# Block products in the first feed-forward: weight sums that only add, two of four per group made by accumulating transfers

## The chip, the cores and the metric

The kernel runs on one core of one Trainium2 chip. The metric is the device time of one execution in microseconds. Three runs of the kernel before took 991.48, 992.41 and 993.05 us; the median is 992.41 us.

## What is computed

One decoder layer on 512 tokens of width 1024, all in float32: a SwiGLU feed-forward, a token mixer (pooling and dilated attention, gated), a second SwiGLU feed-forward, a final norm. Each of the three is modulated by shifts, scales and gates that come from a condition vector `c` and a 1024 x 9216 matrix. Cut to what matters here:

```python
def swiglu(u, w_in, w_out):
    a, b = jnp.split(u @ w_in, 2, axis=-1)      # w_in 1024 x 5632, w_out 2816 x 1024
    return (jax.nn.silu(a) * b) @ w_out

mod = cond @ w_ada[l] + b_ada[l]                # nine vectors of 1024
u = modulate(rmsnorm(h, g_norm_ffn1[l]), sh1, sc1)
h = h + 0.5 * gt1 * swiglu(u, w_ffn1_in[l], w_ffn1_out[l])
...                                             # token mixer
u = modulate(rmsnorm(h, g_norm_ffn2[l]), sh3, sc3)
h = h + 0.5 * gt3 * swiglu(u, w_ffn2_in[l], w_ffn2_out[l])
return rmsnorm(h, g_final)
```

The change concerns `u @ w_in` of the first feed-forward.

## The kernel before

**Three matmuls for one.** Activations stand transposed (features on partitions, 512 tokens along the row). A float32 number is split into two parts of the type fp32r, `hi` (rounded) and `lo` (the rest), for weights and activations alike, and a product is the sum of `hi*uh`, `hi*ul` and `lo*uh` (`mm3`, L373, and `product`, L758). Every weight is loaded once as a tile of 128 x up to 1024 numbers (512 KB), its `hi` is written by ScalarE (ACT, L331) and its `lo` by VectorE (DVE, L343) into two rings, and TensorE (PE) reads them there.

**Seven products for eight.** For most of `u @ w_in` the kernel takes two column tiles of `a` and two of `b` together, as a group (`duo`, L771). The weights of a group are a 2 x 2 matrix of blocks: the upper and lower half of the 1024 features by `a` and `b`; the activations are a 2 x 2 matrix too, feature halves by token halves. By Winograd's form of Strassen's product seven block products do the work of eight, at the price of sums. Four sums of weight blocks are made per group (from r11, r12, r22, r21), and four sums of activation blocks once per feed-forward (`u_steps`, L717, kept split as `S`). Seven products of 24 matmuls (128 x 256) follow one another on three banks A, B and C; after some of them ACT copies a bank away (L774) before a later product goes on in the same bank: after product 0 it copies A to C, and product 2 writes A again. The banks and these copies are put together at the end (L807, L831), then silu (L790) and the multiplication (L793).

**Stages.** The first feed-forward has 22 tile pairs: 0 to 3 are computed at the start while the norm is still being built, 4 and 5 by plain products, and 6 to 21 as eight groups, two in each of four parts. After each part comes a part of `w_out` (L908 on; L923 adds its result to `H` on DVE). Beside them DVE computes the modulation vectors, one 128 x 1024 product and sum per 128 numbers (`bg`, L419, and L402); their matrix comes in by the same transfers. The mixer has three groups of its own (`gate_duo`), which the change leaves alone. The second feed-forward has nine groups.

**Order.** The order is written out by hand (`manual_schedule`). `plan` (L203) makes one list of all weight tiles in the order of use. An entry names what is to be split: a loaded tile (`raw`), or one of two sum tiles (`x`, two quarters of the tile `X`), and if it is a sum, from which two tiles. `blocks` makes the seven entries of a group. `look` (L353) is called before each product and splits up to three or four entries ahead; `split_hi` issues the sum (`make`, L262, the DVE instruction at L268) and ACT's copy, `split_lo` the DVE subtraction. Each engine works through its own instructions in this order, and waits at the first one that is not ready. SyncE (SP) issues the loads (L251) as buffers become free; in this stage these are three `raw` tiles and two quarters of `X`.

**Two forms of the sums.** `blocks` has a flag. Without it (first feed-forward and mixer) all four sums are DVE instructions: x0 = r12 - r11, x1 = r22 - x0, r12 = r22 - r12, x0 = r21 - x1. With it (second feed-forward) all are additions: x0 = r12 + r11 and x1 = r22 + x0 on DVE, and r12 += r22 and x1 += r21 in place by transfers with addition, issued from GpSimd's queue (POOL, `add`, L272 to L276). The first is issued right behind the making of x1, the second behind the split of r21. The signs are made good by other signs in the activation sums (`u_steps`, L739 to L744) and in the copies and sums behind the products (`sign` and `add`, L775, L807, L822, L828, L831). POOL has no other work in the first feed-forward; it computes the pooling in the mixer and part of the final norm.

Of the kernel before, what the change touches and what calls it, by code (L numbers as in the profile page):

```python
# [12 lines left out]
OP = mybir.AluOpType  # L13
# [126 lines left out]
def chunk_widths():  # L140
    outs = [D] * (KT // 2 * (len(PARTS) - 1)) + [(FT - PARTS[-1][0]) * P] * KT
    f1 = [2 * FIRST * P] * KT + [D] * (2 * (FT - FIRST)), outs
    mix = [D] * 24 + [4 * P] * 2 + ([D] * 4 + [4 * P] * 2) * (KT // 2 - 1) + [D] * KT
    return f1, mix, ([D] * (2 * FT), outs)


class Kernel:
# [6 lines left out]
    def plan(self):  # L154
        (i1, o1), mix, (i2, o2) = chunk_widths()
        self.chunks = []
        for name, ws in (("wf1i", i1), ("wf1o", o1), ("wmix", mix), ("wf2i", i2), ("wf2o", o2)):
            off, rec = 0, []
            for w in ws:
                rec.append((name, off, w))  # L160
                off += P * w
            self.chunks.append(rec)
        f1i, f1o, mx, f2i, f2o = self.chunks


        self.loads, self.order, self.last = [], [], {}
        self.shifted, self.adds = set(), {}

        def plain(recs):
            for r in recs:  # L170
                n = len(self.loads)
                self.loads.append(r)
                self.last[n] = len(self.order)
                self.order.append((r[2], n, ("raw", n), None))

        def blocks(recs, plus=False):
            n = len(self.loads)
            i = len(self.order)
            self.shifted.update(range(len(self.order), len(self.order) + 7))
            self.loads.extend(recs)  # L180
            r11, r12, r22, r21 = (("raw", n + i) for i in range(4))
            x0, x1 = ("x", 0), ("x", 1)
            add = OP.add if plus else OP.subtract
            x2 = x1 if plus else x0
            if plus:
                self.adds[i + 2], self.adds[i + 3] = (r12, r22, True), (x1, r21, False)
            for need, src, make in ((0, r11, None), (1, x0, (x0, r12, r11, add)), (2, x1, (x1, r22, x0, add)), (3, r21, None),
                                    (3, r12, (r12, r22, r12, not plus and add)), (3, r22, None),
                                    (3, x2, (x2, r21, x1, not plus and add))):
                for j, x in enumerate((r11, r12, r22, r21)):  # L190
                    if x == src or (make and x in make):
                        self.last[n + j] = len(self.order)
                self.order.append((D, n + need, src, make))

        def shift(i):

            self.shifted.update(range(len(self.order) - i, len(self.order)))

        def ffn(n, ins, outs, first):
            j, at = first, 0  # L200
            if first:
                plain(ins[:KT])
                at = KT  # L203
            for part, (k0, k1) in enumerate(PARTS):
                while j < pairs_before(n, part):
                    if j < PLAIN[n]:
                        plain(ins[at:at + 2])
                        if n and j < 2:
                            shift(2)
                        j, at = j + 1, at + 2  # L210
                    else:
                        blocks(ins[at:at + 4], n == 2)
                        j, at = j + 2, at + 4
                plain(outs[part * KT // 2:(part + 1) * KT // 2] if part + 1 < len(PARTS) else outs[-KT:])

        ffn(0, f1i, f1o, FIRST)
        shift(4)
        base = len(self.order)
        plain(mx[:26])
        for i in range(26, len(mx) - KT, 6):  # L220
            blocks(mx[i:i + 4])
            plain(mx[i + 4:i + 6])
        plain(mx[-KT:])
        self.shifted.update(range(base, base + 4))
        shift(3)
        ffn(2, f2i, f2o, 0)
        shift(5)
        self.fetched = self.done = self.made = 0

        self.ready = True  # L230
        self.pos, self.held, self.retired, self.half = 0, None, [], None

        self.small, self.smalls = None, []
        self.at, self.start, self.top = {}, {}, 0
        self.buf = {}
        self.units = {base + i: 2 * P for i in (4, 5)}
        self.units.update({base + i: T for i in range(16, 20)})
# [34 lines left out]
    def add(self, i, made):  # L272

        if i in self.adds and self.adds[i][2] == made:
            o, x = (self.source(z) for z in self.adds[i][:2])
            self.nc.gpsimd.dma_start(o, x, accum_op=OP.add)  # L276
# [440 lines left out]
    def u_steps(self, n):  # L717

        nc, v = self.nc, self.nc.vector
        (a11, a12), (a21, a22) = self.U4  # L720

        def add(o, x, y, op):
            return lambda: v.tensor_tensor(o, x, y, op=op)

        def split(i, u):
            x = u if i < 3 else u.rearrange("p (k t) -> p k t", k=4)
            parts = [lambda: nc.scalar.activation(self.S[i][0], x, AF.Copy),
                     lambda: v.tensor_tensor(self.S[i][1], x, self.S[i][0], op=OP.subtract)]
            return parts if n else lambda: [f() for f in parts]

        def whole(u, k):
            x = slice(k, k + 4)
            hi, lo = (y.rearrange("p (k t) -> p k t", k=KT)[:, x, :HT] for y in (self.UHv, self.ULv))
            return lambda: v.tensor_tensor(u.rearrange("p (k t) -> p k t", k=4), hi, lo, op=OP.add)

        def minus(o, x, y):
            return lambda: v.scalar_tensor_tensor(o, x, -1.0, y, op0=OP.mult, op1=OP.subtract)

        if n:  # L739
            adds = [add(a22, a22, a21, OP.subtract), add(a21, a11, a21, OP.subtract), minus(a11, a22, a11),  # L740
                    minus(a12, a12, a11)]
        else:
            adds = [add(a22, a21, a22, OP.add), add(a21, a11, a21, OP.subtract), add(a11, a22, a11, OP.subtract),
                    add(a12, a12, a11, OP.subtract)]  # L744
        return ([whole(a11, 0), whole(a12, 4)] if n else []) + adds, [split(2, a21), split(1, a11), split(0, a22), split(3, a12)]

    def step(self):
# [23 lines left out]
    def duo(self, n, j, first, last, extra):  # L771

        nc, v = self.nc, self.nc.vector
        copy = lambda o, x, f=1.0: nc.scalar.activation(o, x, AF.Copy, scale=f)  # L774
        sign, add = (-1.0, OP.subtract) if n else (1.0, OP.add)  # L775
        T1, T2 = slice(0, HT), slice(HT, T)
        blk = lambda ks, t: [(self.UH[k][:, t], self.UL[k][:, t]) for k in ks]
        lo4, hi4 = range(4), range(4, 8)
# [5 lines left out]
        A, B, C = self.nb(), self.nb(), self.nb()  # L784
        s = self.fw.tile([P, 2 * T], F32, name="sl")
        c = self.fw.tile([P, 2 * T], F32, name="hf")
        u2, u3, p5 = (self.fw.tile([P, T], F32, name=x) for x in ("u2", "u3", "p5"))
        q = lambda x: x.rearrange("p (j h t) -> p j h t", j=2, h=2)
        r = lambda x: x.rearrange("p (j t) -> p j t", j=2)
# [13 lines left out]
        for i, (bank, u, start) in enumerate(((A, blk(lo4, T1), True), (B, S[0], True), (A, S[1], False),  # L803
                                              (C, blk(hi4, T1), False), (A, S[2], False), (B, S[3], False),
                                              (A, blk(hi4, T2), False))):
            if i == 6:
                v.tensor_tensor(q(c)[:, :, 1, :], r(u3), r(p5), op=add)  # L807

            late = i == 2 and n == 0 and j == PLAIN[0]
            if not late:  # L810
                self.look(4)
            self.product(bank, u, start, 0 if i else extra)
            self.step()
            if i == 0:
                copy(C, A)
                if first:
                    first()
                    self.free += self.rawx[:1]
            elif i == 1:
                copy(p5, B)  # L820
            elif i == 2:
                copy(u2, A, sign)  # L822
                if late:
                    self.look(3)
            elif i == 3:
                silu(0, C)
            elif i == 4:
                copy(u3, A, sign)  # L828
            elif i == 6:
                silu(1, A)  # L830
                v.tensor_tensor(q(c)[:, :, 0, :], r(u2), r(B), op=add)  # L831
        if last:
            mult()
            high()
# [983 lines left out]
```

## Time and profile before

| | |
|---|---|
| median of three runs | 992.41 us |
| profiled execution | 992.0 us |
| its span, first to last instruction | 990.2 us |
| granted TensorE clock | 0.999 |
| busy: PE, DVE, ACT, POOL | 979.9, 764.6, 474.6, 45.5 us |
| groups of the first feed-forward | 103.7 to 321.6 us of the span |
| groups of the second feed-forward | 709.4 to 946.4 us |
| transfers with addition | 18, from 697.0 us on |

The profile is one execution, recorded instruction by instruction. Times are microseconds from the first instruction. PE is TensorE's matmuls and PEld its weight loads, which overlap them. A row of a window gives busy time and count of instructions per engine; a row of a timeline gives start, duration, engine, line and operation, output and inputs, and in brackets how long the engine stood idle before and what let it go on. "DMA to landing" runs from the issue of a transfer until its data is there. The line numbers are those of the kernel before.

### The profile page before, as it was taken

How to read it: one execution, taken by the hardware profiler on the slowest of the kernel's cores; microseconds unless marked ns; L12 is line 12 of the kernel's file. 1: busy time of each engine (PE TensorE's matmuls, PEld its weight loads, DVE VectorE, ACT ScalarE, POOL GpSimd, SP SyncE). 2: the span in 40 equal slices, each digit the busy share in tenths (PEclk: the TensorE clock that was granted, in tenths of full speed). 3: DMA queues.
4: the chain of work that ended last, by engine and by line, in shares of the span. 5: the costliest groups of instructions: out<-in, count | busy, mean ns of one | idle time of the engine just before them, and what ended most of it. 6: DMA issues, size and time to landing. Idle time of an engine off the chain costs nothing.

```text
span 990.2 us, 16423 instructions
## 1 busy us (share of the span) xinstructions
PE 979.9 (99%) x6688; PEld 892.8 (90%) x6688; DVE 764.6 (77%) x1072; ACT 474.6 (48%) x712; POOL 45.5 (5%) x49
## 2 busy tenths in 40 slices
PE   8999999999999999999999999999999999999997
PEld 7888998989999899888879998998899898998997
DVE  7989979889797677888879877768676667566653
ACT  5453553525445553446545552455355254352553
POOL 0000000000000000006200000000010000000002
PEclk9999999999999999999999999999999999999999
DMA  9856445465563416654243326513576365563512
GB/s 345 277 184 241 150 149 178 163 192 160 186 205 105 141 57 194 229 184 161 68 122 111 107 81 212 175 44 106 145 194 174 88 175 140 128 184 80 152 34 86
DMA packets 47470, 151.19 MB, mean 153 GB/s; under 512 B 6561, under 2 KB 9377, under 8 KB 47394
## 3 DMA queue, kind: packets, MB, share of 16 engines
q1 hardware_dynamic: 44224, 140.18, 43.4%
q0 software_dynamic: 2592, 9.44, 5.5%
q8 instruction: 52, 0.85, 0.4%
q10 hardware_dynamic: 578, 0.53, 0.2%
q14 instruction: 24, 0.20, 0.1%
HBM read 135.29 MB, written 2.24 MB: 139 GB/s over the span
## 4 chain that ended last, share of the span: by engine, by line
PE 94%; DVE 2%; DMA 1%; SPq 1%; issue 1%; ACT 0%; POOL 0%; POOLq 0%; DVEq 0%; ACTq 0%
PE bank L375 15%; PE bank L376 15%; PE bank L377 15%; PE bank L769 13%; PE bank L768 13%; PE bank L767 13%; PE bank L1744 1%; PE bank L1748 1%; PE bank L1746 1%; SPq L1076 1%; PE bank L1420 1%; PE bank L1122 1%; PE bank L1173 1%; DMA H<-xT 1%; PE bank L1421 1%
## 5 line engine op out<-in xcount | busy, mean ns | idle before, releaser
L343 DVE TENSOR_TENSOR wlo<-raw,whi 128x1024 fp32r<-128x1024 f32 (+4 forms) x162 | 170.6, 1065 | 60.0 <-ACT whi L331 59.8
L767 PE MATMUL bank<-UH,whi 128*128 128x256 f32 x640 | 176.7, 276 | 0.0
L768 PE MATMUL bank<-UL,whi 128*128 128x256 f32 x640 | 176.7, 276 | 0.0
L769 PE MATMUL bank<-UH,wlo 128*128 128x256 f32 x640 | 176.7, 276 | 0.0
L331 ACT ACTIVATE whi<-raw 128x1024 fp32r<-128x1024 f32 (+4 forms) x162 | 146.2, 921 | 39.6 <-DVE raw L268 33.0
L375 PE MATMUL bank<-HI,whi 128*128 128x512 f32 (+1 forms) x406 | 146.2, 360 | 0.0
L376 PE MATMUL bank<-HK,whi 128*128 128x512 f32 (+1 forms) x406 | 145.9, 359 | 0.0
L377 PE MATMUL bank<-HI,wlo 128*128 128x512 f32 (+1 forms) x406 | 145.8, 359 | 0.0
L343 DVE TENSOR_TENSOR wlo<-X,whi 128x1024 fp32r<-128x1024 f32 (+3 forms) x104 | 111.9, 1083 | 39.6 <-ACT whi L331 39.4
L767 PEld LDWEIGHTS bank<-UH,whi 128*128 128x128 f32 x640 | 120.1, 188 | 0.4
L768 PEld LDWEIGHTS bank<-UL,whi 128*128 128x128 f32 x640 | 120.2, 188 | 0.0
L769 PEld LDWEIGHTS bank<-UH,wlo 128*128 128x128 f32 x640 | 120.1, 188 | 0.0
L767 PE MATMUL bank<-SH,whi 128*128 128x256 f32 x408 | 112.6, 276 | 0.0
L768 PE MATMUL bank<-SL,whi 128*128 128x256 f32 x408 | 112.6, 276 | 0.0
L769 PE MATMUL bank<-SH,wlo 128*128 128x256 f32 x408 | 112.6, 276 | 0.0
L331 ACT ACTIVATE whi<-X 128x1024 fp32r<-128x1024 f32 (+3 forms) x104 | 95.7, 943 | 24.9 <-DVE X L268 23.9
L375 PE MATMUL bank<-UH,whi 128*128 128x512 f32 (+1 forms) x304 | 105.6, 348 | 0.0
L376 PE MATMUL bank<-UL,whi 128*128 128x512 f32 (+1 forms) x304 | 104.2, 343 | 0.1
L377 PE MATMUL bank<-UH,wlo 128*128 128x512 f32 (+1 forms) x304 | 104.0, 342 | 0.0
L377 PEld LDWEIGHTS bank<-HI,wlo 128*128 128x128 f32 x406 | 76.2, 188 | 11.6
L375 PEld LDWEIGHTS bank<-HI,whi 128*128 128x128 f32 x406 | 76.2, 188 | 11.5
L376 PEld LDWEIGHTS bank<-HK,whi 128*128 128x128 f32 x406 | 76.3, 188 | 11.3
(350 smaller groups left out, 1831.0 us busy)
## 6 DMA issues: line engine op xcount, KB each, us to landing
raw<-wmix SPq DMA_DIRECT2D x44, 512.0 KB, 3.8
raw<-wf1i SPq DMA_DIRECT2D x31, 512.0 KB, 4.6
raw<-wf2i SPq DMA_DIRECT2D x30, 512.0 KB, 4.0
ada<-wada SPq DMA_DIRECT2D x23, 512.0 KB, 5.5
AR<-wada SPq DMA_DIRECT2D x19, 512.0 KB, 4.4
X<-wf2i SPq DMA_DIRECT2D x14, 512.0 KB, 4.1
cs<-wada SPq DMA_DIRECT2D x12, 512.0 KB, 3.7
X<-wf1i SPq DMA_DIRECT2D x12, 512.0 KB, 4.4
```

What stands on the lines that cost most here:

```text
L331: self.nc.scalar.activation(self.hi[:, y], r[:, x], AF.Copy)
L343: self.nc.vector.tensor_tensor(self.lo[:, y], r[:, x], self.hi[:, y], op=OP.subtract)
L375: M(ps, hi, uh, start=start, stop=False)
L376: M(ps, hi, ul, start=False, stop=False)
L377: M(ps, lo, uh, start=False, stop=stop)
L767: M(o, hi, uh, start=start and p == 0 and k == 0, stop=False, skip_group_check=True)
L768: M(o, hi, ul, start=False, stop=False, skip_group_check=True)
L769: M(o, lo, uh, start=False, stop=k == 3, skip_group_check=True)
L1076: nc.sync.dma_start(w[32 * o:32 * o + 32], t[32 * i:32 * i + 32])
L1122: nc.tensor.matmul(S[:, o], q[:, toks], k[:, ks], start=True, stop=True, skip_group_check=True)
L1173: self.nc.tensor.matmul(self.bO[64 * h:64 * h + 64, P * hp:P * hp + P], x, pt[:, (2 * h + j) * P:(2 * h + j + 1) * P], start=j == first, s ...
L1420: M(b, uh, hi, start=k == 0, stop=False)
```

## The change

The flag of `blocks` is set for the first feed-forward as well, and the signs there follow, so that the two feed-forwards have one form. The number of products, the loads, the order of the list and the splits stay as they are.

```diff
 def plan(self): ... def ffn(n, ins, outs, first):
-                        blocks(ins[at:at + 4], n == 2)
+                        blocks(ins[at:at + 4], True)

 def u_steps(self, n):
-        if n:
-            adds = [add(a22, a22, a21, OP.subtract), add(a21, a11, a21, OP.subtract), minus(a11, a22, a11),
-                    minus(a12, a12, a11)]
-        else:
-            adds = [add(a22, a21, a22, OP.add), add(a21, a11, a21, OP.subtract), add(a11, a22, a11, OP.subtract),
-                    add(a12, a12, a11, OP.subtract)]
+        adds = [add(a22, a22, a21, OP.subtract), add(a21, a11, a21, OP.subtract), minus(a11, a22, a11), minus(a12, a12, a11)]

 def duo(self, n, j, first, last, extra):
-        sign, add = (-1.0, OP.subtract) if n else (1.0, OP.add)
-                v.tensor_tensor(q(c)[:, :, 1, :], r(u3), r(p5), op=add)
+                v.tensor_tensor(q(c)[:, :, 1, :], r(u3), r(p5), op=OP.subtract)
-                copy(u2, A, sign)
+                copy(u2, A, -1.0)
-                copy(u3, A, sign)
+                copy(u3, A, -1.0)
-                v.tensor_tensor(q(c)[:, :, 0, :], r(u2), r(B), op=add)
+                v.tensor_tensor(q(c)[:, :, 0, :], r(u2), r(B), op=OP.subtract)
```

What the flag does in `blocks`, `make` and `add` (not changed):

```python
add = OP.add if plus else OP.subtract
x2 = x1 if plus else x0
if plus:
    self.adds[i + 2], self.adds[i + 3] = (r12, r22, True), (x1, r21, False)
for need, src, make in ((0, r11, None), (1, x0, (x0, r12, r11, add)), (2, x1, (x1, r22, x0, add)), (3, r21, None),
                        (3, r12, (r12, r22, r12, not plus and add)), (3, r22, None),
                        (3, x2, (x2, r21, x1, not plus and add))):
...
self.nc.gpsimd.dma_start(o, x, accum_op=OP.add)
```

## Prediction

> **What bounds the kernel now.** I read the busy times first, then what TensorE waited for, then the windows over the span.
>
> ```profile
> span 990.2 us, 16423 instructions
> PE 979.9 (99%) x6688; PEld 892.8 (90%) x6688; DVE 764.6 (77%) x1072; ACT 474.6 (48%) x712; POOL 45.5 (5%) x49
> ```
>
> TensorE is busy for 979.9 of 990.2 us, so only 10.3 us of the span can be won without fewer or faster matmuls. The windows tell where those 10.3 us lie. Their columns are the stretch, its length, then busy us (x instructions) of PE, PEld, DVE, ACT and POOL, the granted clock, the DMA share and GB/s.
>
> ```profile
> 97.00:143.00 46.00, 46.00 (x373) 44.65 (x372) 41.50 (x43) 26.27 (x34) 0.00 (x0) 1.00 0.48 152
> 143.00:203.00 60.00, 60.00 (x435) 56.24 (x434) 52.35 (x62) 26.91 (x36) 0.00 (x0) 1.00 0.52 171
> 203.00:263.00 60.00, 60.00 (x435) 56.24 (x434) 53.67 (x71) 26.73 (x36) 0.00 (x0) 1.00 0.56 176
> 263.00:323.00 60.00, 60.00 (x435) 56.23 (x434) 50.97 (x64) 26.38 (x37) 0.00 (x0) 1.00 0.49 154
> 323.00:350.00 27.00, 27.00 (x174) 24.39 (x173) 18.20 (x27) 13.28 (x20) 0.00 (x0) 1.00 0.40 122
> 350.00:362.00 12.00, 11.87 (x104) 11.67 (x103) 10.26 (x26) 6.66 (x15) 0.00 (x0) 1.00 0.24 72
> 362.00:650.00 288.00, 287.42 (x1909) 253.40 (x1908) 233.82 (x390) 143.70 (x250) 24.39 (x20) 1.00 0.45 143
> 768.00:828.00 60.00, 60.00 (x435) 56.23 (x434) 38.90 (x40) 26.68 (x35) 3.07 (x5) 1.00 0.51 139
> 828.00:888.00 60.00, 60.00 (x435) 56.23 (x434) 38.94 (x41) 26.79 (x36) 3.49 (x5) 1.00 0.54 141
> 888.00:948.00 60.00, 60.00 (x435) 56.23 (x434) 37.34 (x40) 25.12 (x34) 3.41 (x4) 1.00 0.47 122
> ```
>
> Two things are to be seen. The eight groups of the first feed-forward lie in 103 to 322 us, and there TensorE has no idle time at all: 46.00 of 46.00, then three times 60.00 of 60.00 us. From 350 to 650 us it is idle for 0.13 + 0.58 = 0.71 us; the rest of the 10.3 us stands at the two ends of the program. And the last three rows are the second feed-forward, where the form that is now to come to the first one already runs: the same 435 matmuls in 60 us, with DVE busy for 37 to 39 us in place of 51 to 54. VectorE's load does not set TensorE's pace here.
>
> **The change part by part.** In the instruction lists of the two programs, engine by engine, PE, ACT and SP have the same instructions in the same order. DVE loses 16 adds, POOL gains 16 transfers, two DVE instructions change their kind; nothing else moves, no weight load either.
>
> *Weight sums.* Eight groups lose two 128x1024 adds each.
>
> ```profile
> L268 DVE TENSOR_TENSOR X<-raw,X 128x1024 f32<-128x1024 f32 x23 | 28.1, 1220 | 0.2
> L723 DVE TENSOR_TENSOR X<-X x6: 1218/1224/1225, 56.3 to 673.1; 128x1024 f32<-128x1024 f32 x6
> L737 DVE SCALAR_TENSOR_TENSOR X<-X x2: 1216/1216/1216, 678.7 to 680.9; 128x1024 f32<-128x1024 f32 x2
> ```
>
> DVE loses 16 x 1.22 = 19.5 us of 764.6. What of it lay on the path: nothing, since no wait for DVE shows as TensorE idle in 97 to 350 us. Term: 0.
>
> *Input sums and signs.* Two of four sums become the form of L737, 1216 for 1224 ns: 0. The scale of -1 and the subtractions replace equal operations: 0.
>
> *The 16 added transfers.* The second feed-forward has 18 of them, which gives the price.
>
> ```profile
> L276 POOL DMA_DIRECT2D X<-raw x7: 859/869/882, 726.0 to 925.4; - x7
>   ACT whi L331: 2.8, 1
> DMA to landing us min/median/max: 4.5/5.4/7.3
> q0 software_dynamic: 2592, 9.44, 5.5%
> 444.21 0.11 POOL L1239 MEMSET tr<- 128x16 f32 x1 [443.76 <-DMA rt<-tr]
> ```
>
> POOL gains 16 x 0.87 = 13.9 us while it stands idle: until 444.21 us it has nothing but the four constants at the start, so no queue is passed that anyone waits for. A landing takes 4.5 to 7.3 us where DVE took 1.22. The new wait is ACT's: its high-part copy (L331) of the fifth and seventh weight of a group now waits for a landing, and behind it in ACT's queue stand the copies of the banks (L774) that later products wait for. Such a wait shows once among the 18, 2.8 us, and TensorE did not feel it. So the cover must be counted group by group, the tightest first: the very first group, where the splits run least ahead.
>
> ```profile
> 99.66 1.21 DVE L268 TENSOR_TENSOR X<-raw,raw 128x1024 f32<-128x1024 f32 x1
> 102.05 2.50 DVE L343 TENSOR_TENSOR wlo<-X,whi 128x1024 fp32r<-128x1024 f32 x2
> 105.79 1.22 DVE L268 TENSOR_TENSOR raw<-raw,raw 128x1024 f32<-128x1024 f32 x1
> ...
> 107.12 1.07 ACT L331 ACTIVATE whi<-raw 128x1024 fp32r<-128x1024 f32 x1 [2.88 <-DVE raw L268]
> 108.09 0.58 ACT L774 ACTIVATE bank<-bank 128x512 f32<-128x512 f32 x1
> 112.89 1.06 ACT L331 ACTIVATE whi<-X 128x1024 fp32r<-128x1024 f32 x1 [0.26 <-DVE X L268]
> ...
> 109.12 0.28 PE L767 MATMUL bank<-SH,whi 128*128 128x256 f32 x1
> ```
>
> Before, the add at 105.79 let ACT go at 107.12; the bank copy ended at 108.09 + 0.58 = 108.67, and the third product, which writes that bank again, began at 109.12: a margin of 0.45 us. After, the transfer may be issued once the first sum has read its tile, at 99.66 + 1.21 = 100.87. How soon POOL follows, and when ACT is let go, the second feed-forward shows.
>
> ```profile
> 717.78 1.22 DVE L268 TENSOR_TENSOR X<-raw,raw 128x1024 f32<-128x1024 f32 x1
> 719.36 1.23 DVE L343 TENSOR_TENSOR wlo<-raw,whi 128x1024 fp32r<-128x1024 f32 x1 [0.36 <-ACT whi L331]
> ...
> 697.04 1.04 POOL L276 DMA_DIRECT2D raw<-raw  x1 [219.23 <-DMA raw<-wf2i]
> 719.56 0.85 POOL L276 DMA_DIRECT2D raw<-X  x1 [16.76 <-DVE X L268]
> ...
> 702.72 1.06 ACT L331 ACTIVATE whi<-raw 128x1024 fp32r<-128x1024 f32 x1 [2.77 <-DMA raw<-raw]
> ```
>
> The sum of 717.78 ended at 719.00, the issue is at 719.56: 0.56 us. So here the issue is at 101.43. From issue to ACT it took 702.72 - 697.04 = 5.68 us for the first transfer of that stage. That lets ACT go at 107.11, where it went at 107.12: stall 0. By the fastest landing (4.5) it is 105.9, stall 0; by the slowest (7.3) it is 108.73, the copy follows 0.97 us later as before (107.12 to 108.09), ends at 110.28, and TensorE waits 1.2 us. A gain is excluded, as there is no idle time to win. I take 0, the row nearest in kind (first transfer of a stage, a weight load in flight), and keep 0 to 1.2 us.
>
> The same group's second transfer follows the low parts that end at 102.05 + 2.50 = 104.55: issued by 105.1, landed by 112.4 at the slowest, and ACT wants it at 112.89. Stall 0. The later groups have more room; one as a sample.
>
> ```profile
> 232.99 1.22 DVE L268 TENSOR_TENSOR X<-raw,X 128x1024 f32<-128x1024 f32 x1
> 239.03 1.23 DVE L343 TENSOR_TENSOR wlo<-X,whi 128x1024 fp32r<-128x1024 f32 x1 [0.27 <-ACT whi L331]
> ...
> 243.39 1.14 ACT L331 ACTIVATE whi<-raw 128x256 fp32r<-128x256 f32 x2
> 248.89 1.05 ACT L331 ACTIVATE whi<-X 128x1024 fp32r<-128x1024 f32 x1
> 251.11 0.60 ACT L774 ACTIVATE u<-bank 128x512 f32<-128x512 f32 x1 [1.17 <-PE bank L769]
> ```
>
> The first transfer lands by 234.21 + 0.56 + 7.3 = 242.1 for a use at 243.39, the second by 240.26 + 0.56 + 7.3 = 248.1 for 248.89; beyond that ACT is idle for 1.17 us before its next bank copy. Stall 0 even at the slowest landing seen.
>
> *DMA traffic.* One added transfer takes 5.5% of 990.2 us / 18 = 3.0 us of all 16 engines. Four in 60 us raise the share from 0.49 to 0.56 up to some 0.69 to 0.76, above what the second feed-forward shows with its transfers (0.47 to 0.54). A weight load beside one may land up to 3.0 us later; outside the first group that is within the lead. In the first group it would meet the same 0.45 us margin, so its bound is that of the stall above and is not added again.
>
> **Sum.** 0 + 0 + 0, with 0 to +1.2 us for the first group. The profiled execution took 992.0 us (span 990.2 and 1.8 us around it), the median of the three runs is 992.41, 0.4 above. The forecast is the median, **992.4 us**.
>
> **Rivals.**
>
> *Slower: the first group's transfer is issued or written late, and TensorE waits behind ACT.* From 99 us DVE runs without a break; if POOL could write its transfer only in DVE's next pause, that is once the low part at 106.92 and the two output sums after it are done in the new order, about 108.3 us. Then ACT goes at 108.3 + 5.7 = 114.0, the bank is copied by 115.5, and TensorE waits 115.5 - 109.1 = 6.4 us: **998.8**. It decides from a release of ACT after about 107.5 us (109.12 - 0.58 - 0.97, and a little for the signal). Only the first group is so tight. Against it speaks the pair of rows at 719: POOL's issue at 719.56 took 0.85 us within a DVE add of two inputs that ran from 719.36 to 720.59.
> The Trainium skill ("SBUF — State Buffer", the box on the "DVE blocks DMA" trap) says that transfers issued from POOL starve while DVE runs an operation in a 2-port mode, and that two-input operations hold the port only against a POOL operation that reads SBUF. By that rule these adds, all of two inputs, do not starve the transfer, and the row at 719.56 agrees.
>
> *Faster: less VectorE work lets TensorE run closer.* It could be a faster pace of matmuls with less traffic beside them, or an earlier end of a wait. For the pace nothing speaks: 435 matmuls take 60 us with DVE at 53.67 and at 37.34. For waits, all that VectorE could give back up to 650 us is 0.71 us: **991.7**, which still counts as no change. More than that could come only from something the trace does not show.
>
> *The change does nothing that counts.* This is the forecast itself: VectorE gets its 19.5 us, off the path.
>
> **How the numbers follow.** 0.2% is 2 us, about what a measurement of this kernel can tell from no change. The forecast (stall 0 to 1.2 us) has a chance of 0.86; the first rival, with stalls of over 2 us in the first group or late loads elsewhere, 0.10; the second, beyond 2 us, 0.04, for causes unseen. These are also the chances of same, slower and faster. Range: from the lowest of the three runs shown (991.48) less a little for the 0.71 us that could come back, 991.2; up to the highest run (993.05) plus the 1.2 us, 994.3. Outside lie the 0.14 of the two rivals.
>
> **What would show it.** Right: DVE near 745 us and POOL near 59; PE busy in 97 to 350 us without idle time; the first group's third product at 109.1 us, as now; ACT let go by a transfer near 107.1. Wrong: the product at 109.12 starts later, by so much as the copy of the bank before it is late (stall), or the 60 us windows hold fewer than 435 matmuls (pace or loads). A gain of more than 1 us would mean that the pace of matmuls depends on VectorE after all.

## The result, and the profile after

The changed kernel took 993.57 us (median of 17 runs, 993.12 to 997.68), the kernel before 991.30 us beside it (17 runs, 990.92 to 993.05): a ratio of 1.0028, 95% interval 1.0021 to 1.0036. It is slower by 2.27 us: the interval leaves out "no difference", and the loss is a little over the 0.2% that the forecast took for no change. The time lies in the range that was forecast; the claim of "no difference" does not hold. The three runs of before that the forecast started from had a median of 992.41 us, 1.1 us above that of the 17.

These are the two page lines of the changed kernel's profiled execution (994.49 us) that answer to those of before.

```profile
span 992.7 us, 16475 instructions
PE 981.5 (99%) x6688; PEld 893.8 (90%) x6688; DVE 747.6 (75%) x1056; ACT 473.9 (48%) x712; POOL 59.4 (6%) x65
```

The work went where the diff sends it: DVE lost 764.6 - 747.6 = 17.0 us and POOL gained 13.9 us. The span grew by 2.5 us all the same. The windows of the same execution show where; their columns are as before (the stretch, its length, busy us of PE, PEld, DVE, ACT, POOL, then the granted clock, the DMA share and GB/s).

```profile
97.00:143.00 46.00, 44.46 (x365) 43.26 (x364) 35.91 (x38) 25.16 (x32) 3.62 (x4) 1.00 0.72 193
143.00:203.00 60.00, 60.00 (x434) 56.23 (x434) 48.02 (x59) 26.66 (x35) 3.47 (x4) 1.00 0.71 204
203.00:263.00 60.00, 60.00 (x434) 56.22 (x433) 49.24 (x67) 26.58 (x35) 3.47 (x4) 1.00 0.73 212
263.00:323.00 60.00, 60.00 (x434) 56.22 (x433) 47.10 (x60) 26.72 (x39) 3.46 (x4) 1.00 0.68 190
```

Only the first row lost: 46.00 - 44.46 = 1.54 us of TensorE's time, where before it had none idle. That row holds the first two groups with four of the 16 added transfers. The twelve of the next three rows cost TensorE nothing: it was busy for 60.00 of 60.00 us three times, although the DMA share rose from about 0.5 to 0.7. The lost time is one gap. It stands in two timelines of the changed kernel (start, duration, engine, line, operation; in brackets the idle time before and what ended it), PE's first:

```profile
108.26 0.28 PE L764 MATMUL bank<-SH,wlo 128*128 128x256 f32 x1
110.07 0.38 PE L762 MATMUL bank<-SH,whi 128*128 128x256 f32 x1 [1.54 <-ACT bank L769]
```

```profile
108.48 1.06 ACT L331 ACTIVATE whi<-raw 128x1024 fp32r<-128x1024 f32 x1 [4.94 <-DMA raw<-raw]
109.44 0.58 ACT L769 ACTIVATE bank<-bank 128x512 f32<-128x512 f32 x1
```

The matmul at 110.07 begins the first group's third product (L762 here is L767 of before; the copy of the bank, L774, is L769). From 108.26 it came 1.81 us later where 0.11 is the rule, so the gap is 1.70 us (the 1.54 us are the part of it in which no earlier matmul was still running). TensorE waited for ACT's copy of the bank, and the copy stood in ACT's queue behind the split of the fifth weight, which waited for the first added transfer. The chain of waits that leads there, of the same execution:

```profile
100.77 7.60 DMA raw<-raw
108.37 0.02 issue
108.39 0.04 ACTq L331
...
108.64 0.81 issue
109.44 0.59 ACT bank L769
```

The transfer was issued at 100.77, 0.60 us after the sum that frees its tile, and took 7.60 us to land. From its issue to ACT's start at 108.48 that is 7.71 us; the forecast had taken 5.68.

The span's 2.5 us are thus put together, as the two profiled executions show them: the stage began 0.7 us earlier than in the execution before, and the stall and the first matmul after it cost 1.8; between 362 and 380 us the matmuls of 256 columns came every 117.8 ns instead of 113.3, +0.6; the end, from the last DVE operation to the last instruction, took 5.37 instead of 4.56 us, +0.8. The first is not owed to the transfers: in e3 below, which has none of them in this stage, the first matmul that reads `SH` begins at 105.70 us, in the changed kernel at 105.65, in the profiled execution of before at 106.40. The pace looks like chance: of the thirteen kernels below, the profiled execution of one (e6) is slower there too, that of another (e5) from 108 to 143 us, and eleven at neither place. The stall and the end are what the experiments went after.

### The profile page after: what moved, and what is told of

It is laid out like the page before. It is cut to its first block, busy times and chain, and to the rows that moved or that the text cites. A ratio compares the mean times of both kernels' runs of the same rounds, so it can differ in the third digit from the quotient of the medians.

```text
span 992.7 us, 16475 instructions
## 1 busy us (share of the span) xinstructions
PE 981.5 (99%) x6688; PEld 893.8 (90%) x6688; DVE 747.6 (75%) x1056; ACT 473.9 (48%) x712; POOL 59.4 (6%) x65
## 4 chain that ended last, share of the span: by engine, by line
PE 85%; DVE 8%; issue 2%; ACT 1%; DMA 1%; SPq 1%; POOL 0%; POOLq 0%; ACTq 0%; DVEq 0%
PE bank L375 14%; PE bank L376 13%; PE bank L377 13%; PE bank L762 13%; PE bank L764 13%; PE bank L763 13%; DVE ada L402 2%; DVE wlo L343 2%; DVE UL L506 1%; SPq L1070 1%; PE bank L1414 1%; PE bank L1116 1%; PE bank L1167 1%; DMA raw<-raw 1%; PE bank L1415 1%
## 5 line engine op out<-in xcount | busy, mean ns | idle before, releaser
L762 PE MATMUL bank<-UH,whi 128*128 128x256 f32 x640 | 176.7, 276 | 0.0
L762 PEld LDWEIGHTS bank<-UH,whi 128*128 128x128 f32 x640 | 120.1, 188 | 0.4
L762 PE MATMUL bank<-SH,whi 128*128 128x256 f32 x408 | 112.7, 276 | 1.5 <-ACT bank L769 1.5
```

The source lines that it names most:

```text
L762: M(o, hi, uh, start=start and p == 0 and k == 0, stop=False, skip_group_check=True)
```

## Experiments

Theory A: the first group's bank copy stands behind ACT's wait for the first added transfer, and nothing else costs. Rival B: the traffic of all 16 transfers. Rival C: the changed signs. Later came D, the end of the program, and the question why the first transfer is late. Each kernel was measured beside the kernel before; a ratio is to it, with its 95% interval in brackets. The "gap" is the delay of the first group's third product, beyond the 0.11 us from one matmul to the next; the "end" is the time from the last DVE operation to the last instruction. Both come from one profiled execution of each kernel. Line numbers of these kernels are up to five higher than those of the changed kernel.

### Which transfers cost, and do the signs

Three kernels come from one diff with three conditions. A sum named in `dve` is made by a DVE addition (in lines left out here), the others by transfer.

```diff
             if plus:
-                self.adds[i + 2], self.adds[i + 3] = (r12, r22, True), (x1, r21, False)
+                if 0 not in dve:
+                    self.adds[i + 2] = (r12, r22, True)
+                if 1 not in dve:
+                    self.adds[i + 3] = (x1, r21, False)
...
-                        blocks(ins[at:at + 4], True)
+                        blocks(ins[at:at + 4], True, (0, 1) if n == 0 and j == PLAIN[0] else ())   # e1
+                        blocks(ins[at:at + 4], True, (0, 1) if n == 0 and j > PLAIN[0] else ())    # e2
+                        blocks(ins[at:at + 4], True, (0, 1) if n == 0 else ())                     # e3
```

e1, the first group's two sums on DVE:

> The changed kernel, but the first group's two in-place sums are VectorE additions again (15 of 16 signs and sums as changed, 14 transfers left). Theory A, the first group's bank copy stands behind ACT's wait for the first transfer: the third product starts on time, no TensorE gap at 110 us, time of the kernel before (about 991.3 us, ratio 1.000). Rival B, the 16 transfers cost by their traffic all along the stage: 7/8 of the loss stays, about 993.3 us, ratio 1.002. Rival C, the other sums and signs cost: 993.6 us, ratio 1.0023.

Measured: 991.83 us (11 runs), before 991.52; ratio 1.0005 [0.9996, 1.0013]. There is no gap.

e2, only the first group's two by transfer:

> The reverse: only the first group's two sums are transfers, the other seven groups use VectorE additions. Theory A: the whole loss, a TensorE gap of 1.5 to 2 us before the first group's third product, about 993.6 us, ratio 1.0023 to 1.0028. Rival B: 1/8 of the loss, about 991.6 us, ratio 1.0003. Rival C: 993.6 us but without a gap there.

Measured: 993.70 us (9 runs), before 991.52; ratio 1.0026 [1.0016, 1.0036]. The same chain stands in ACT's and PE's timelines of e2:

```profile
108.08 1.06 ACT L334 ACTIVATE whi<-raw 128x1024 fp32r<-128x1024 f32 x1 [4.57 <-DMA raw<-raw]
109.05 0.58 ACT L772 ACTIVATE bank<-bank 128x512 f32<-128x512 f32 x1
```

```profile
108.14 0.28 PE L767 MATMUL bank<-SH,wlo 128*128 128x256 f32 x1
109.68 0.38 PE L765 MATMUL bank<-SH,whi 128*128 128x256 f32 x1 [1.26 <-ACT bank L772]
```

e3, all 16 sums on DVE, with the changed signs:

> The changed signs and activation sums, but all 16 in-place sums are VectorE additions (no transfer with addition in the first feed-forward). Theories A and B: the time of the kernel before, ratio 1.000, TensorE without a gap in 103 to 322 us. Rival C: the full loss, ratio 1.0023 or more.

Measured: 991.12 us (11 runs), before 991.52; ratio 0.9997 [0.9988, 1.0006]. There is no gap.

e2's gap is 1.43 us. Two transfers of one group bring it, fourteen others do not; the signs cost nothing that can be measured. B and C fall, but for one thing: e1's profile shows the long end, 5.38 us, and e2's and e3's the short one (4.56, 4.57). That became theory D.

### ACT's order alone

e4 changes no transfer; in the first group ACT copies the bank ahead of the split that waits:

```diff
-                self.look(4)
+                self.look(3 if i == 0 and n == 0 and j == PLAIN[0] else 4)
             self.product(bank, u, start, 0 if i else extra)
...
                 copy(C, A)
+                if n == 0 and j == PLAIN[0]:
+                    self.look(3)
```

> The changed kernel with two ACT instructions exchanged: in the first group the copy of bank A to C stands ahead of the high part of the fifth weight, which waits for the transfer. All 16 transfers stay. Theory A: the gap is gone, ratio 1.000 to the kernel before, and the high part is still let go near 108.4 us. Rival B: nothing changes, ratio 1.0023 or more. Should TensorE then wait for the fifth weight itself, its product (114 us) would start late; its low part should end near 111, so no.

Measured: 992.20 us (11 runs), before 991.52; 1.0006 [0.9997, 1.0014]. ACT's timeline of e4:

```profile
105.84 0.58 ACT L769 ACTIVATE bank<-bank 128x512 f32<-128x512 f32 x1 [2.04 <-PE bank L764]
107.98 1.06 ACT L331 ACTIVATE whi<-raw 128x1024 fp32r<-128x1024 f32 x1 [1.55 <-DMA raw<-raw]
```

The transfer is as late as ever, ACT is let go at 107.98, and no gap is left, since the copy is done at 106.42. So the lateness costs only through the order of ACT's queue. The median stays 0.7 us over before, which fits the long end (5.37 us); the interval of the ratio does not exclude that there is no difference.

e5 takes away only the first of the two transfers (the condition of e1 with `(0,)` for `(0, 1)`):

> The changed kernel, with only the first group's first in-place sum (r12, the one that the fifth weight waits for) on VectorE; its second sum and the other 14 stay transfers. Theory A, the wait for this one transfer holds up the bank copy: no TensorE gap before the third product, time as in the run with both sums on VectorE, 991.8 to 992.2 us. Rival: the second transfer, or the first group's traffic, has a part in it: a gap stays, about 993 us.

Measured: 991.94 us (11 runs), before 991.27; 1.0009 [1.0000, 1.0018]. There is no gap, ACT is let go at 106.56, and the end takes 5.33 us. The gap is the first transfer's. In its profiled execution the matmuls of 108 to 143 us came every 117.8 ns, the pace by chance named above.

### The end of the program

e6 and e7 are e4 with instructions that do nothing of use, each with its own of the two lines below:

```diff
                 copy(C, A)
+                if n == 0:
+                    v.memset(self.pad[:, :1], 0.0)          # e6, DVE, 8 in all
+                    for _ in range(3):
+                        nc.gpsimd.memset(self.pad[:, :1], 0.0)   # e7, GpSimd, 24 in all
```

> The kernel with the bank copy first, with one more tiny memset (128x1, into an unused tile) on VectorE in each of the first feed-forward's eight groups. It asks for the 0.7 us that the kernels with 14 or 16 transfers have left (991.8 to 992.2 against 991.1 without transfers), which their traces show after the last store: one of its 16 landings is 1.1 us late, beside an 8 KB packet of the instruction queue. Theory D, VectorE's shorter instruction stream has moved its fetch to the end: eight instructions more move it away again, 991.2 us, last store to end 4.6 us in place of 5.4. Otherwise (GpSimd's longer stream, or the transfers themselves): 992.2 us, 5.4 us.

Measured: 991.34 us (11 runs), before 991.27; 1.0003 [0.9994, 1.0012]. The end takes 4.48 us.

> The kernel with the bank copy first, with 24 more tiny memsets (128x1) on GpSimd in the first feed-forward. Theory E, GpSimd's longer instruction stream has moved its fetch into the last stores: 24 instructions more move it to an earlier place, 991.2 us, last store to end 4.6 us. Theory D (VectorE's stream) or a cost of the transfers themselves: 992.2 us and 5.4 us as without them.

Measured: 992.03 us (11 runs), before 991.27; 1.0008 [0.9999, 1.0016]. The end takes 5.37 us.

Eight more instructions on DVE made the end 0.89 us shorter than in e4, twenty-four on GpSimd left it as it was. The medians of e6 and e7 are 0.7 us apart, which fits, though their intervals overlap. The DMA view from the last DVE operation to the end shows what lies beside the stores (queue, packets, MB, share; then the stores issued in it, with the time to landing), of the changed kernel and of e6:

```profile
q14 instruction: 2, 0.02, 0.9%
issues: line engine op xcount, KB each, median us to landing
out_dram<-out ACTq DMA_DIRECT2D x2, 128.0 KB, 2.3
out_dram<-out SPq DMA_DIRECT2D x1, 128.0 KB, 3.5
```

```profile
q14 instruction: 1, 0.01, 0.7%
issues: line engine op xcount, KB each, median us to landing
out_dram<-out ACTq DMA_DIRECT2D x2, 128.0 KB, 2.2
out_dram<-out SPq DMA_DIRECT2D x1, 128.0 KB, 2.4
```

SP's last store lands after 3.5 us instead of 2.4. The packet records show what comes with it: in the changed kernel an 8 KB packet of the instruction queue starts 2.13 us after the last DVE operation, among the last stores' packets, and one of that store's 16 landings is 1.1 us behind the others. In all 15 kernels of this study the two go together: with a packet of that queue at 2.12 to 2.17 us the end takes 5.33 to 5.38 us, with none before 4.0 us it takes 4.48 to 4.57. So some 0.8 us of the loss, by the traces, do not come from the transfers' work but go with a piece of code that is fetched while the last results are stored. What sets the packet's place was not settled: eight instructions more on DVE moved it, twenty-four on GpSimd did not, and the held load of e12, below, moved it too.

### Why the first transfer is late

There were three guesses. The first is that a queue's first use is slow: e8 sends two tiny transfers ahead, at 94.32 and 95.82 us, the transfer in question following at 100.76.

```diff
                         ...
+                        if n == 0 and part == 0 and m == 0:
+                            nc.gpsimd.dma_start(self.pad[:, 16 * i:16 * i + 16], self.H[i][:, :16], accum_op=OP.add)
```

> The changed kernel, with two tiny transfers with addition (128x16, into an unused tile) from GpSimd's queue some 5 us ahead of the first group's first. In the changed kernel that one's first packet came 2.6 us after its issue, later ones' mostly 1.4 us. If the queue's first use after a pause is what costs, the first packet comes at 1.4, ACT is let go 1.1 us earlier and the gap falls from 1.7 to about 0.6 us: 992.5 us. If the weight load issued 0.57 us before is what holds it up, or the transfer's length, nothing changes: 993.6 us.

Measured: 993.66 us (7 runs), before 991.27; 1.0025 [1.0014, 1.0037]. The transfer came no sooner (ACT let go at 108.81), and the guess falls. But this execution showed what the stall can cost besides. Windows of e8, around the gap, after it, and later:

```profile
108.00:112.00 4.00, 2.13 (x14) 1.93 (x13) 1.87 (x2) 3.19 (x5) 0.00 (x0) 0.85 0.39 77
110.80:114.20 3.40, 3.40 (x18) 3.40 (x18) 2.75 (x4) 2.04 (x4) 0.00 (x0) 0.50 0.60 165
114.20:118.00 3.80, 3.80 (x35) 3.80 (x34) 1.38 (x2) 2.68 (x4) 0.00 (x0) 0.99 0.87 304
```

TensorE was idle for 1.87 us in this gap. Behind it the granted clock was 0.50 for some 3.4 us: 18 matmuls there, 35 in the 3.8 us that follow; each took 213 ns instead of 113, which is another 1.6 us. The gap of the changed kernel's profiled execution, 1.54 us idle, did not halve the clock. Its 17 runs fall into ten of 993.12 to 993.61 and seven of 994.49 to 997.68 us. A halved clock is not what sets the seven apart: the profiled execution is one of them (994.49), and three of them were granted 0.999 on average, as much as any run here, where 3.4 us at half would take 0.0017 off. What made them longer stays open. The Trainium skill ("TensorE: Matmul & The Clock Gate", "Part 1: The HAM clock gate") says that the clock falls to half after an idle window of about 3.4 us, and that this window runs freely. The 3.4 us at half clock agree with that; the idle time does not, for 1.87 us were enough in this execution.

The second guess is that PE's instruction fetch (a 16 KB packet at 101.57 that held one DMA engine for 2.30 us in the changed kernel) delays one of the sixteen parts. The third is that the weight load does it that SP issues 0.57 us ahead, at 100.20 in SP's timeline of the changed kernel:

```profile
98.44 0.33 SPq L251 DMA_DIRECT2D X<-wf1i  x1
100.20 10.95 SPq L251 DMA_DIRECT2D raw<-wf1i  x2
```

e9 was to move the load, e10 the fetch, e11 both.

```diff
             if hold:
+                self.last[n] = i + 3        # e9 and e11: keep the tile that the load is to fill
...
-        warm(5, self.ones)
+        warm(14, self.ones, 16)             # e10 and e11: 36 more PE instructions at the start
```

> As the changed kernel, but the buffer that the first group's first added transfer reads is kept three tiles longer, so that the load of the next weights on SyncE's queue (issued at 100.20 in the changed kernel, half a microsecond ahead of the transfer) is issued some 5 us later, about 106. The orders of ACT, DVE and PE are unchanged. Theory 'the load beside it': the transfer of 100.77 lands after about 5.5 us instead of 7.6, ACT is let go by about 106.4, the third product's gap is under 0.3 us, time about 992.0 (the tail of 0.8 us stays). Theory 'instruction fetch': the 16 KB packet of the PE queue near 101.5 keeps one DMA engine busy for 0.9 to 2.3 us whatever the load does; the last landing stays 6.9 to 7.6 us after the issue, the gap stays about 1.0 to 1.7 us, time about 993.5. Were it both, something between: last landing 6 to 6.8 us.

Measured: 994.55 us (8 runs), before 991.18; 1.0031 [1.0020, 1.0041]. The edit missed its aim: the load was still issued 0.57 us ahead of the transfer, for SP issues it when the last reader of its buffer is through, not where the code asks for it. The transfer took 6.64 us, a little under its repeats in the kernels so far (6.86 to 7.94), and the gap was 1.05 us. That the median is nevertheless 1 us above the changed kernel's 993.57 was not explained; its eight runs lie between 992.71 and 996.54.

> As the changed kernel, but the five warming products of the start (20 instructions on PE) are fourteen narrow ones (56 instructions), so that every later instruction of PE stands 36 places further on in its stream, and the 16 KB packet of PE's instruction queue that came at 101.57 comes about 4 us earlier, near 97.5, ahead of both the load of 100.20 and the transfer of 100.77. The work from the norm on is the same. Theory 'instruction fetch': the sixteen landings of the first transfer lie within 0.7 us instead of 2.2, the last comes about 5.9 us after the issue, the gap at the third product is under 0.4 us, time about 992.0 (tail of 0.8 us stays). Theory 'the load beside it': landing stays at 6.9 to 7.6 us, gap 1.0 to 1.7 us, time about 993.5.

Measured: 998.81 us (5 runs), before 991.18; 1.0074 [1.0060, 1.0087]. The narrow products made the start 4 us longer, so the total says nothing of the fetch; the first group does. Its transfer's flight in the DMA view of e10 (queue, packets, MB, share):

```profile
q0 software_dynamic: 224, 0.85, 57.4%
q1 hardware_dynamic: 208, 0.72, 40.2%
issues: line engine op xcount, KB each, median us to landing
raw<-raw POOLq DMA_DIRECT2D x1, 512.0 KB, 7.5
```

No instruction queue is among them, and it still took 7.5 us, with a gap of 1.65 us. The fetch is not needed for the lateness.

> The later load and the earlier instruction fetch together. By either theory, and by both at once, the first transfer's last landing is at 5.0 to 5.9 us after the issue, there is no gap at the third product, time about 991.9 to 992.1 with the tail of 0.8 us. If the gap stays here at over 1 us, neither the load nor the fetch is what makes the transfer late.

Measured: 997.45 us (5 runs), before 991.18; 1.0062 [1.0050, 1.0075]. The landing took 7.30 us, the gap was 1.35 us. Its load had not moved either, so it repeats e10.

What spoke for the load was a count over the large transfers of the kernels so far: the time to the last landing by the share of DMA time that other packets took between 1.4 and 4.4 us after the issue. Here it is for all 393 of the thirteen kernels before e12 (worked out from the packet records):

```
share of other packets   transfers   mean us to last landing
under 0.1                   274          5.2
0.1 to 0.3                   70          6.3
0.3 to 0.5                   33          6.9
0.5 to 0.7                   12          7.3
0.7 and over                  4          7.9
```

The single transfers spread widely around these means: with under 0.1 beside them they took 4.5 to 7.2 us, and the slowest of all took 8.9 (e1's at 116.08, without a gap behind it).

e12 holds the load truly back. To e9's edit it adds one more write to the tile that the load fills (`kept` notes which):

```diff
             self.nc.gpsimd.dma_start(o, x, accum_op=OP.add)
+            if i in self.kept:
+                self.nc.gpsimd.memset(self.buf[self.kept[i]][:, :1], 0.0)
```

> As the changed kernel, but the load that comes half a microsecond ahead of the first added transfer is truly held back: its buffer gets one more write, a one-column memset on GpSimd behind the issue of the first group's second transfer, so that the load can't be issued before about 105 (100.20 in the changed kernel; the earlier try to hold it left it at 101.10, since SyncE issues a load when the last reader of its buffer ends and not when the code asks for it). Theory 'the load beside it': over all transfers of the runs so far the last landing goes from 5.2 us (other packets on under a tenth of the DMA time between 1.4 and 4.4 us after the issue) to 7.2 (half to seven tenths); with the load gone from that stretch the first transfer's last landing comes 4.6 to 5.6 us after its issue, ACT is let go by about 106.5, no gap at the third product, time 991.9 to 992.3 with the 0.8 us tail (ratio about 1.0008). Theory 'something of the first transfer itself' (its place, its buffers): the landing stays at 6.6 to 7.6 us, the gap at 1.0 to 1.8 us, time 993.5 to 994.5.

Measured: 991.53 us (11 runs), before 991.24; 1.0004 [0.9995, 1.0013]. SP's and ACT's timelines of e12:

```profile
98.98 0.33 SPq L254 DMA_DIRECT2D X<-wf1i  x1
105.69 3.95 SPq L254 DMA_DIRECT2D raw<-wf1i  x2
```

```profile
106.60 1.06 ACT L336 ACTIVATE whi<-raw 128x1024 fp32r<-128x1024 f32 x1 [2.53 <-DMA raw<-raw]
107.57 0.58 ACT L774 ACTIVATE bank<-bank 128x512 f32<-128x512 f32 x1
```

The load went from 0.57 us ahead to 4.39 us behind, the transfer landed after 5.20 us instead of 7.60, ACT was let go at 106.60, and the gap is gone. The DMA view over the first transfer's flight, of the changed kernel, of e12, and of the kernel before over the flight that the forecast took for its price (from 697.04 on):

```profile
q0 software_dynamic: 239, 0.91, 61.2%
q1 hardware_dynamic: 213, 0.74, 32.6%
q8 instruction: 1, 0.02, 1.9%
```

```profile
q0 software_dynamic: 167, 0.62, 63.1%
q1 hardware_dynamic: 41, 0.10, 5.0%
q8 instruction: 1, 0.02, 1.2%
```

```profile
q0 software_dynamic: 144, 0.52, 46.9%
q1 hardware_dynamic: 156, 0.55, 33.5%
q14 instruction: 1, 0.01, 0.3%
```

q1 carries the weight loads, q0 the added transfers. Loads of 0.74 MB beside the transfer gave 7.60 us (all of them started in its first 5.58 us), 0.10 MB gave 5.20, and in the row of before 0.55 MB gave 5.58. The fetch on q8 is there in e12 too. That the first transfer is late only with the load beside it is shown. How late is not a simple sum, since the last of 16 landings counts and they spread: over 2.19 us in the changed kernel, 0.71 in e12, 0.66 in the row of before.

The row of before has a load just as close ahead, at 696.47 in SP's timeline of before, 0.57 us before the transfer of 697.04:

```profile
696.47 0.33 SPq L251 DMA_DIRECT2D raw<-wf2i  x1
```

That transfer, the first of the second feed-forward, is in all 15 traces, and its landing took 4.53 to 7.21 us. The 4.53 is e12's, where no load packet ran between 1.4 and 4.4 us after the issue. The 7.21 is e7's, with 0.36 MB of loads in that stretch; before took 5.58 with as much. So the load makes such a transfer late, but its amount does not say by how much, and the 5.58 was one draw of many. What spreads the sixteen landings stays open.

e13 has e12's held load and e6's eight memsets:

> The held load of the run before and the eight one-column DVE memsets that brought the tail back to 4.48 us with the bank copy put first. If the late first transfer (by the load beside it) and the tail are all that the change costs, both are gone here with all sixteen transfers in place: no gap at the third product, 4.5 us from the last DVE operation to the end, time 991.0 to 991.5, no difference from before (ratio 0.9995 to 1.0003). If the sixteen transfers cost something besides, it stays above by that.

Measured: 991.30 us (11 runs), before 991.24; 1.0003 [0.9994, 1.0012]. There is no gap, the landing took 4.92 us and the end 4.48 us. The end was short in e12 already. With both causes gone, 16 transfers in place of 16 DVE sums make no difference that can be measured, and no version here is measurably faster than the kernel before.

## Why the prediction was wrong, point by point

- **TensorE has no idle time in the groups, VectorE's load does not set its pace.** Right. DVE's 17 us bought nothing: e13, with all transfers and no stall, stands at 1.0003, e3, with all sums on DVE, at 0.9997.
- **Weight sums and signs at 0.** Right, by e3.
- **POOL's queue, the issue, the later groups at 0.** Right: POOL 59.4 us busy against the forecast's 59; issue 0.60 us after the sum against 0.56; 60.00 of 60.00 us in three windows, although later transfers of the changed kernel landed up to 8.02 us after their issue.
- **The first group's stall: 0, bound +1.2 us. Here it failed.** "From issue to ACT it took 702.72 - 697.04 = 5.68 us for the first transfer of that stage ... I take 0, the row nearest in kind (first transfer of a stage, a weight load in flight)." The path, the margin and the place were as said; the landing was mis-sized. The landing took 7.60 us, above even the slowest of the 18 (7.3); from issue to ACT it was 7.71 us, and the stall was 1.70 us, above the bound (in e8 2.03 us). e12 shows that the load beside it was needed for that: without it the landing took 5.20 us and there was no stall. The row had a load beside it too and was still fast. It was one execution of a transfer that took 4.53 to 7.21 us in the 15 traces, and it carried 0.55 MB of weights beside it where there are 0.74 MB here. That this amount alone makes 7.60 of 5.58 us is not shown. The error lies in taking one row as the price of a term with 0.45 us to spare.
- **DMA traffic: "its bound is that of the stall above and is not added again".** This let the error stand. It asked how much later a load lands beside a transfer, not how much later the transfer lands beside a load, which was the question for the one transfer with 0.45 us to spare. The traffic itself was forecast well: a share of 0.69 to 0.76, measured 0.68 to 0.73.
- **Not in the sum at all:** the end of the program, +0.8 us in the profile (e6 and e13 without it, e1 and e4 with it alone at 0.3 and 0.7 us over before); and the half clock behind a gap (seen in e8, not in the changed kernel's profile). Stall and end, 1.70 and 0.81 us in the traces, are about the 2.27 us that were measured.
- **The slower rival** had the path (ACT held back, bank copy, third product) and the point from which it decides (ACT let go after about 107.5; it was 108.48), but not the cause: POOL's transfer did not wait for a pause of DVE. The transfer of e12 landed in 5.20 us while DVE was busy almost throughout, as this window over 3 us of its flight shows.

```profile
102.70:105.70 3.00, 3.00 (x28) 2.96 (x27) 2.94 (x5) 1.37 (x2) 0.97 (x2) 1.00 0.92 173
```

- **The starting point.** 992.4 us was the median of three runs; 17 runs gave 991.30. By the forecast's own sum, 991.30 with 0 to 1.2 us on top, 993.57 would have been outside. It fell into the range by luck: the upper end was reckoned from the highest of the three runs (993.05), and that margin covered a stall that was too small and an end that was not in the sum.
- **What was to show it wrong did:** "the product at 109.12 starts later, by so much as the copy of the bank before it is late". It started at 110.07 in a stage that had begun 0.7 us earlier.

## What to carry to other kernels

A DVE operation of 1.2 us that becomes a transfer of 4.5 to 8.9 us, as in these traces, is free only where everything queued behind its reader can wait as long: find the tightest reader, look at what stands behind it in its engine's queue, and price the transfer by the slowest landing with as much load traffic beside it as there is at that place, from several executions rather than from one row. The cures are cheap: put what the bottleneck waits for ahead of the waiting instruction (e4), or hold back the load that collides with the transfer (e12). And here, where TensorE is busy 99% of the span, 17 us taken off DVE bought nothing, so there was only something to lose.

## What the runs showed of the hardware

- A fetch of instructions moves as DMA packets beside the data. With one 8 KB packet among the last stores, a landing of these came 0.8 to 1.1 us behind the others and the end was 0.8 to 0.9 us longer, in all eight kernels that had it there and in none of the seven that did not.
- After 1.87 us without a matmul TensorE's clock was halved for about 3.4 us (e8); after idle times of 0.88 to 1.54 us in five other kernels it was not. So a stall can cost nearly twice its length. These are single executions, and they do not give a threshold.
- A transfer with addition of 512 KB, at the same place of the same code, took 4.53 to 7.21 us to land in 15 traces (the first of the second feed-forward).
- SyncE issues a load when its buffer's last reader ends; asking for it later in the code did not delay it, one more write to the buffer did (issued 0.57 us ahead of the transfer in e9, at 101.10, and 4.39 us behind it in e12, at 105.69).
- The matmuls of 256 columns came every 113.3 ns, and in some executions every 117.8 ns for stretches of tens of microseconds, with the same code there (108 to 143 us in e5, 362 to 380 us in the changed kernel and in e6).
